# Maximum over the last axis of a 64 MB array: another division into loads, and another share for GpSimd

## The chip, the core and the metric

One core of a Trainium2 chip runs the kernel. The metric is the device time in microseconds (us) of one execution, as the median of several runs; lower is better. A profile of one execution, with a trace of every instruction and of every transfer, stands beside it.

## The reference

```python
# x: (32, 512, 1024) float32
def reference(x):
    return np.max(x, axis=-1).astype(np.float32)     # out: (32, 512)
```

The 32 x 512 vectors make 16384 rows of 1024 numbers, 67.1 MB in all; each gives one maximum. There is nearly nothing to compute per byte.

## The kernel before, in words

**Blocks and loads.** The 16384 vectors are cut into 128 blocks: a block puts one vector on each of the 128 partitions, 1024 numbers wide (512 KB). In this text a "row" of a load is one such block. `BLOCKS` (L13) divides the 128 rows into loads: a first list that sums to 112 rows, and a second whose sum is 14; the last two rows are loaded as four pieces (`PIECES`, L26, two column ranges for each of two rows). SyncE issues all of them in order on one queue (L238 and L243), into a ring of 47 rows in SBUF (`RING`, L17). A load is issued once everything that reads the rows it overwrites stands in the program ahead of it, and on the chip it waits until these reads are done. Loads are numbered from 0; load 10, for instance, is the one of 7 rows.

**VectorE** does most of the work: `maximum` (L78) is one reduce along the columns. Step `dK` reduces the rows of load K that VectorE keeps for itself, straight into the result columns.

**GpSimd's share.** For a few rows near the end the columns are turned, so that GpSimd can take the maximum over the partitions. `SHARED` (L20) says for a load K: (m, parts), so of its last m rows the first `parts` column-blocks of 128 go this other way. A chunk holds as many rows as fit eight column-blocks. Step `tN` handles chunk N: TensorE transposes each 128x128 block into PSUM (L160), ScalarE copies the result to SBUF (L166), GpSimd takes the maximum over the partitions (L168). Step `bN` turns the first partition's row back into columns with TensorE (L178). Where `parts` is below 8, step `pK` lets VectorE reduce the remaining columns of those rows beside it, in PSUM, and step `mK` takes the maximum of both. The loads named in `RANK` (L22) share one PSUM tile, `joint`, with one merge at the end (`m99`): so that each row of `joint` has as many columns, `partial` (L194) splits the remaining columns of a row into `s` segments and leaves one maximum for each. `joint` is as wide as its widest load needs: `parts`, plus one where `parts` is below 8.

**The end.** Steps `f0` to `f3` reduce the four pieces; the second piece of a row takes the result of the first in with it. Then `m99`. Results of the first 112 rows are stored once `f0` is done, the last 16 after `m99`.

**Order.** `PLAN` (L31) is the order of all steps, written out by hand. `in_turn` (L71) makes each engine keep it. Pools hold two buffers each for the transposes in PSUM, for their copies and for GpSimd's results, so chunk N waits for buffers of chunk N-2; the tile `joint` also makes TensorE and VectorE wait for one another where both write it.

Of the kernel before, what the change touches and what calls it, by code (L numbers as in the profile page):

```python
# [8 lines left out]
F32 = mybir.dt.float32  # L9

BLOCKS = [  # L13
    [2, 15, 16, 14, 11, 11, 10, 10, 8, 8, 7],
    [3, 3, 3, 2, 1, 1, 1],
]
RING = 47  # L17


SHARED = {10: (3, 8), 13: (2, 3), 14: (2, 3), 17: (1, 2)}  # L20

RANK = {13: 1, 14: 2, 17: 2}  # L22

PIECES = [(532, 492), (592, 432)]  # L26

PLAN = """  # L31
    d0 d1 d2 d3 d4 d5 d6 d7 d8 d9 t0 d10 t1 t2 d11 b0 d12 b1 d13 t3 p13 b2 p14 t4 m10 d15 b3
    d16 p17 t5 f0 b4 f1 f2 b5 f3 m99
""".split()

NOSYNC = mybir.DependencyInfo(mybir.DependencyClass.NoSync, mybir.DependencyReason.DATA)
# [4 lines left out]
def kernel(  # L41
# [35 lines left out]
    def maximum(out, in_):  # L77
        return in_turn("DVE", nc.vector.reduce_max(out=out, in_=in_, axis=X))  # L78
# [20 lines left out]
    for sizes in BLOCKS:  # L99
# [7 lines left out]
        b, place = 0, {}  # L107
        for i in sorted(range(len(sizes)), key=lambda i: RANK.get(base + i, 0)):
            place[i] = b
# [8 lines left out]
    assert first == I  # L118
    shared = [SHARED.get(j, (0, C)) for j in range(len(loads))]

    lead = [0 if RANK.get(j) == 3 else n - m for j, ((_, n, _, _), (m, _)) in enumerate(zip(loads, shared))]
    final = [j for j in range(len(loads)) if j in RANK]
    final.sort(key=lambda j: loads[j][3])
# [11 lines left out]
    def rows(j):  # L135
        start, n, _, _ = loads[j]
        return ring[:, I + start * D:I + (start + n) * D].rearrange("p (i d) -> p i d", d=D)
# [4 lines left out]
    def share(j):  # L142
        m, parts = shared[j]
        if j in RANK:
            r = loads[j][3] + lead[j] - col0
            return joint[:, r:r + m, :]
        if j not in fetched:
            got = psmall.tile([P, m, parts + (parts < C)], F32)
            fetched[j] = got
        return fetched[j]  # L150
# [39 lines left out]
    def partial(j):  # L190
        m, parts = shared[j]

        s = width - parts if j in RANK else 1
        maximum(share(j)[:, :, parts:], rows(j)[:, lead[j]:lead[j] + m, parts * P:].rearrange(  # L194
# [102 lines left out]
```

## Time and profile before

| what | value |
| --- | --- |
| median of 3 runs | 163.71 us (163.69 to 163.97) |
| span of the profiled execution, first to last instruction | 162.1 us |
| VectorE busy | 135.3 us (83%), 33 instructions |
| GpSimd busy | 15.9 us (10%), 10 instructions, of them 6 reductions over partitions |
| TensorE matmul busy | 13.6 us (8%), 76 instructions |
| ScalarE busy | 6.3 us (4%) |
| loads and stores | 67.18 MB, 414 GB/s over the span |
| mean granted TensorE clock | 0.955 |

The page gives no time of its own for the profiled execution beside the span; the 1.6 us between span and median lie outside the span.

How to read it: a row of a group names the line, the engine, the operation, output and input with their shapes, and after the bar the busy time in us, the mean of one instruction in ns, and the idle time of the engine just before, with what ended it. The chain of waits follows the work that ended last back in time: each piece has its start, its length and its place. A stretch view gives the busy time of each engine between two moments.

### The profile page before, as it was taken

To read this page: it belongs to the slowest core of one execution; us is meant where nothing else is said; L and a number is where in the kernel's file an instruction comes from. 1 tells how busy PE (TensorE), PEld (TensorE's weight loads), DVE (VectorE), ACT (ScalarE), POOL (GpSimd) and SP (SyncE) were. 2 spreads that over 40 slices of the span, in tenths; PEclk is the share of its full clock that TensorE was granted. 3 is DMA by queue.
4 is the path that set the end of the run, shared out by engine and by line. 5 is a ranking of instruction groups with operands and counts; after the bars stand their busy time and mean duration, and the time that the engine had idled before them with its cause. 6 is when DMAs were issued, how large, how long until landed. Compare 5 with 4: busy or idle time off the path is not lost.

```text
span 162.1 us, 295 instructions
## 1 busy us (share of the span) xinstructions
PE 13.6 (8%) x76; PEld 11.7 (7%) x76; DVE 135.3 (83%) x33; ACT 6.3 (4%) x7; POOL 15.9 (10%) x10
## 2 busy tenths in 40 slices
PE   0000000000000000000000000000000000772942
PEld 0000000000000000000000000000000000762731
DVE  3500019998399999999999999996999999999994
ACT  3000000000000000000000000000000000241120
POOL 0000000000000000000000000000000000099791
PEclk9999999999999999999999999999999999996555
DMA  5995999599879999898999799799999989999991
GB/s 178 566 485 258 470 501 517 259 517 517 354 340 439 453 404 534 356 523 367 478 411 475 334 485 475 334 485 388 477 429 388 466 382 446 415 421 416 411 388 34
DMA packets 3456, 67.18 MB, mean 414 GB/s; under 512 B 640, under 2 KB 896, under 8 KB 1536
## 3 DMA queue, kind: packets, MB, share of 16 engines
q1 hardware_dynamic: 3168, 67.11, 96.8%
q10 hardware_dynamic: 288, 0.07, 0.2%
HBM read 67.11 MB, written 0.07 MB: 414 GB/s over the span
## 4 chain that ended last, share of the span: by engine, by line
DMA 50%; DVE 47%; SPq 1%; issue 0%; DVEq 0%
DMA ring<-in_x_dram 50%; DVE ring L78 45%; DVE joint L78 2%; SPq L238 1%; DVEq L292 0%
## 5 line engine op out<-in xcount | busy, mean ns | idle before, releaser
L78 DVE TENSOR_REDUCE ring<-ring 128x1 f32<-128x1024 f32 (+13 forms) x20 | 129.9, 6547 | 23.5 <-DMA ring<-in_x_dram 23.5
L168 POOL PARTITION_ALL_REDUCE top<-sb x6 | 15.7, 2658 | 142.6 <-ACT sb L166 142.5
L160 PE MATMUL ps<-ident,ring 128*128 128x128 f32 x38 | 9.0, 423 | 140.0 <-DMA ring<-in_x_dram 140.0
L160 PEld LDWEIGHTS ps<-ident,ring 128*128 128x128 f32 x38 | 7.6, 225 | 140.1 <-issue 140.1
L166 ACT COPY sb<-ps 128x1024 f32<-128x1024 f32 (+2 forms) x6 | 5.0, 834 | 150.5 <-PE ps L160 143.5
L78 DVE TENSOR_REDUCE joint<-ring 128x2 f32<-128x1280 f32 (+1 forms) x3 | 3.9, 1314 | 0.0
L178 PE MATMUL got<-ident,top 1*128 1x1 f32 x24 | 2.7, 228 | 3.8 <-POOL top L168 3.6
L178 PEld LDWEIGHTS got<-ident,top 1*128 1x128 f32 x24 | 2.4, 188 | 4.6 <-POOL top L168 4.6
L178 PE MATMUL joint<-ident,top 1*128 1x1 f32 x14 | 2.0, 244 | 1.9 <-POOL top L168 1.9
L178 PEld LDWEIGHTS joint<-ident,top 1*128 1x128 f32 x14 | 1.7, 210 | 2.7 <-POOL top L168 2.7
L166 ACT ACT_TABLE_LOAD x1 | 1.3, 1283 | 0.7 <-PEq L281 0.7
L83 DVE MEMSET ident<- 128x128 f32 x1 | 0.2, 165 | 0.8 <-PEq L281 0.8
L90 DVE TENSOR_SCALAR rowno<-rowno 32x1 f32<-32x1 f32 x3 | 0.4, 146 | 0.1
L85 DVE TENSOR_TENSOR_SCAN colno<-ident 128x128 f32<-128x128 f32 x1 | 0.4, 425 | 0.0
L92 DVE TENSOR_SCALAR ident<-colno,rowno 128x128 f32<-128x128 f32 x1 | 0.3, 288 | 0.0
L87 DVE STREAM_TRANSPOSE rowno<-colno 128x32 f32<-128x32 f32 x1 | 0.2, 211 | 0.0
L78 DVE TENSOR_REDUCE ring<-got 128x3 f32<-128x24 f32 x1 | 0.2, 172 | 0.0
L78 DVE TENSOR_REDUCE ring<-joint 128x5 f32<-128x20 f32 x1 | 0.2, 170 | 0.0
L281 POOL MEMSET const-float32-0.0<- 128x1 f32 x1 | 0.1, 98 | 0.2 <-issue 0.2
L281 POOL MEMSET const-bfloat16-1.0<- 128x1 bf16 x1 | 0.1, 102 | 0.0
L281 POOL MEMSET const-uint8-127<- 128x1 uint8 x1 | 0.1, 101 | 0.0
L281 POOL MEMSET const-float32-1.0<- 128x1 f32 x1 | 0.1, 98 | 0.0
(1 smaller groups left out, 0.1 us busy)
## 6 DMA issues: line engine op xcount, KB each, us to landing
ring<-in_x_dram SPq DMA_DIRECT2D x2, 5632.0 KB, 29.9
ring<-in_x_dram SPq DMA_DIRECT2D x2, 5120.0 KB, 36.8
ring<-in_x_dram SPq DMA_DIRECT2D x2, 4096.0 KB, 32.5
ring<-in_x_dram SPq DMA_DIRECT2D x1, 7680.0 KB, 22.6
ring<-in_x_dram SPq DMA_DIRECT2D x1, 7168.0 KB, 58.0
ring<-in_x_dram SPq DMA_DIRECT2D x3, 1536.0 KB, 35.7
ring<-in_x_dram SPq DMA_DIRECT2D x1, 3584.0 KB, 29.2
ring<-in_x_dram SPq DMA_DIRECT2D x2, 1024.0 KB, 17.8
```

The lines of the kernel that those rows point to most:

```text
L78: return in_turn("DVE", nc.vector.reduce_max(out=out, in_=in_, axis=X))
L83: in_turn("DVE", nc.vector.memset(ident, 1.0))
L85: in_turn("DVE", nc.vector.tensor_tensor_scan(out=colno, data0=ident, data1=ident, initial=-1.0, op0=ALU.add, op1=ALU.mult))
L87: in_turn("DVE", nc.vector.transpose(out=rowno, in_=colno[:, :32]))
L90: in_turn("DVE", nc.vector.tensor_scalar(out=part, in0=part, scalar1=float(q * 32), scalar2=None, op0=ALU.add))
L92: identity = in_turn("DVE", nc.vector.tensor_scalar(out=ident, in0=colno, scalar1=rowno[:, 0:1], scalar2=None, op0=ALU.is_equal))
L160: in_turn("PE", nc.tensor.transpose(out=ps[:, w:w + P], in_=rows(j)[:, lead[j] + r + i, c * P:(c + 1) * P], identity=ident,))
L166: in_turn("ACT", nc.scalar.copy(out=sb[:, :W], in_=ps[:, :W]))
L168: in_turn("POOL", nc.gpsimd.partition_all_reduce(top[:, :W], sb[:, :W], P, bass_isa.ReduceOp.max))
L178: in_turn("PE", nc.tensor.transpose(out=share(j)[:, r + i, c:c + 1], in_=tops[k][0:1, w:w + P], identity=ident[0:1, 0:1],))
L238: load = nc.sync.dma_start(out=rows(issued), in_=src)
L281: nc = _bacc.Bacc("TRN2", target_bir_lowering=False, num_devices=1)
```

## The change

The first list has 10 loads for 11: it starts with 16 rows where there were 2, and ends with 2. The second has 7 loads as before, in other sizes. With the four pieces, 21 transfers stand for 22. GpSimd's share goes from four loads (3x8, 2x3, 2x3 and 1x2 column-blocks, 38 in all) to five (5x3, 4x3, 1x8, 2x3 and 1x2, 43 in all), in eight chunks for six. Load 8, with 8 rows, keeps 3 rows for VectorE alone and has a merge of its own; loads 10, 11, 13 and 16 go to `joint`, which becomes 8 rows of 8 (it was 5 rows of 4), since load 11 shares all eight column-blocks of one row. The segments per row in `partial` become 5, 5 and 6 (they were 1, 1 and 2). The functions stay as they are; ring, pieces and pools too.

In the built program TensorE has 86 transposes (it had 76) and SyncE 21 loads and pieces (22); VectorE has 32 instructions that compute (33).

```diff
 BLOCKS = [
-    [2, 15, 16, 14, 11, 11, 10, 10, 8, 8, 7],
-    [3, 3, 3, 2, 1, 1, 1],
+    [16, 14, 16, 14, 12, 11, 10, 9, 8, 2],
+    [4, 3, 2, 2, 1, 1, 1],
 ]
 RING = 47
-SHARED = {10: (3, 8), 13: (2, 3), 14: (2, 3), 17: (1, 2)}
-RANK = {13: 1, 14: 2, 17: 2}
+SHARED = {8: (5, 3), 10: (4, 3), 11: (1, 8), 13: (2, 3), 16: (1, 2)}
+RANK = {10: 2, 11: 1, 13: 2, 16: 2}
 PIECES = [(532, 492), (592, 432)]
 PLAN = """
-    d0 d1 d2 d3 d4 d5 d6 d7 d8 d9 t0 d10 t1 t2 d11 b0 d12 b1 d13 t3 p13 b2 p14 t4 m10 d15 b3
-    d16 p17 t5 f0 b4 f1 f2 b5 f3 m99
+    d0 d1 d2 d3 d4 d5 d6 d7 d8 t0 t1 t2 p8 b0 d9 t3 b1 p10 b2 t4 t5 m8 d11 b3 d12 b4 p13 t6 d14
+    b5 d15 p16 t7 f0 b6 f1 f2 b7 f3 m99
 """.split()
```

## The prediction, made before the changed kernel ran

> **What bounds the kernel now.** I read the slices of the page first: how busy are the transfers?
>
> ```profile
> span 162.1 us, 295 instructions
> ...
> DMA  5995999599879999898999799799999989999991
> ...
> q1 hardware_dynamic: 3168, 67.11, 96.8%
> q10 hardware_dynamic: 288, 0.07, 0.2%
> ```
>
> The transfers look full with dips. The slices can't say whether a dip is real, so I asked for stretches cut at landings (columns: stretch, its length, busy time and count of PE, PEld, DVE, ACT, POOL, then clock, DMA share, GB/s):
>
> ```profile
> 5.60:23.80 18.20, 0.00 (x0) 0.00 (x0) 2.30 (x2) 0.00 (x0) 0.00 (x0) 1.00 1.01 436
> 23.80:43.10 19.30, 0.00 (x0) 0.00 (x0) 16.14 (x1) 0.00 (x0) 0.00 (x0) 1.00 0.99 428
> 43.10:111.00 67.90, 0.00 (x0) 0.00 (x0) 66.57 (x6) 0.00 (x0) 0.00 (x0) 1.00 0.99 427
> 111.00:139.00 28.00, 0.03 (x1) 0.06 (x1) 27.98 (x3) 0.00 (x0) 0.00 (x0) 1.00 1.00 429
> 139.00:150.00 11.00, 6.93 (x40) 6.42 (x40) 10.96 (x5) 3.04 (x3) 7.95 (x3) 0.89 1.00 422
> ```
>
> The DMA share is 0.99 to 1.01 everywhere: the dips come from packets that straddle slices. **The stream of loads is one unbroken line from the first load to the last piece.** VectorE is nearly as full from 43 us on. The chain of waits shows both:
>
> ```profile
> 1.62 41.49 DMA ring<-in_x_dram
> ...
> 43.13 66.55 DVE ring L78 x5
> ...
> 111.01 38.94 DMA ring<-in_x_dram
> 149.95 0.02 issue
> 149.97 1.22 DVE ring L78
> ...
> 158.57 0.49 DVE ring L78
> 159.05 0.09 issue
> 159.14 0.59 DVE ring L78
> ```
>
> The chain hops between two lines that are both late. After 149.97 it is all VectorE, but the last two piece reduces (158.57, 159.14) follow a landing by about 0.1 us as well.
>
> **The price of a load.** Landings: load 2 (16 rows) at 1.62 + 41.49 = 43.11, load 13 at 111.01 + 38.94 = 149.95; load 1 at 23.76 (VectorE, which waits for it, starts at 23.78, as it starts at 43.13 on load 2). Load 2 takes 19.35 us for 16 rows and one load. From there to load 13 it is 106.84 us for 88 rows and 11 loads. With a per row and b per load, 16a + b = 19.35 and 88a + 11b = 106.84, so a = 1.2047 and **b = 0.075 us**. Load 0 (2 rows) lands at 5.62, so the stream starts, as it were, at 5.62 - 2.48 = 3.14. Before's total, 3.14 + 128 x 1.2047 + 22 x 0.075 = 158.99, meets the last landing (150.0 + 9.0, the last issue's time to landing).
>
> A rule to weigh: the Trainium skill, "DMA: Bandwidth & Descriptors", section "Anatomy of one DMA", gives each DMA a fixed cost of some 2.0 us. By that rule one load fewer would save 2 us. The rows above show it overlapped when loads queue up, so the measured 0.075 is used.
>
> **The stream after the change.** 21 transfers for 22, the bytes unchanged: the last landing moves **by -0.075 us** if the stream stays unbroken. With the same start the 16 rows of the first load land at 22.5, loads 1 to 8 at 39.4, 58.8, 75.7, 90.2, 103.6, 115.7, 126.6 and 136.3, the rest at 138.8, 143.7, 147.4, 149.9, 152.3, 153.6, 154.9, 156.2, the pieces at about 156.9, 157.7, 158.4 and 158.9.
>
> Does a refill come too late? Each load waits for VectorE to leave its rows of the ring. Load 3 waits for reduce 0 (39.7), behind it lies load 2 until 58.8; load 4 for reduce 1 (54.7), behind load 3 until 75.7; loads 5 and 6 for reduce 2 (76.0), with load 4 until 90.2; load 7 for reduce 3 (91.0), with loads 5 and 6 until 115.7; loads 8 to 11 for reduce 4 (103.9); 12 and 13 for reduce 5 (115.7). The least cover is 14 us. The last three loads and the pieces wait for older loads to land; the tightest, the fourth piece, for load 12 at 149.9, with 8 us queued. So the stream holds.
>
> **VectorE.** Its rows:
>
> ```profile
> L78 DVE TENSOR_REDUCE ring<-ring 128x10 f32<-128x10240 f32 x2 | 21.6, 10821 | 1.3 <-DMA ring<-in_x_dram 1.3
> L78 DVE TENSOR_REDUCE ring<-ring 128x1 f32<-128x1024 f32 x3 | 3.6, 1213 | 0.0
> L78 DVE TENSOR_REDUCE joint<-ring 128x2 f32<-128x1280 f32 x2 | 3.0, 1490 | 0.0
> L78 DVE TENSOR_REDUCE joint<-ring 128x2 f32<-128x768 f32 x1 | 1.0, 961 | 0.0
> L78 DVE TENSOR_REDUCE ring<-got 128x3 f32<-128x24 f32 x1 | 0.2, 172 | 0.0
> ```
>
> 1024 more elements cost (10821 - 1213)/9 = 1067.6 ns, 0.96 elements a nanosecond, plus 0.15 us; a queued instruction starts some 0.085 us before the one ahead ends (five of 17.22 + 15.08 + 23.75 + 10.82 = 66.87 fill 66.53). The change removes 5 of 128 column-blocks of 1/8 row, 0.67 us, and starts VectorE's large work at 22.5 for 23.8, but takes away the 2.3 us done at 5.65. In sequence: reduces 0 to 5 end at 39.7, 54.7, 76.0, 91.0, 103.9, 115.7; 6 and 7 wait 0.1 to 0.2 us for landings and end at 126.5 and 136.4. Then load 8: 3 rows 3.35, the share of 5 x 640 columns 3.49; 2 rows 2.28 (145.3); 4 x 640 2.83 (148.0); the merge 0.17; 2 rows twice (152.5). The share of load 13 can start at 152.46, as its load lands (152.3 plus the semaphore); 1.5, 1.21, 1.21, then load 16's share at 156.3, bound by its landing, 0.96; the pieces' two reduces at 157.2 and 157.8; the last two at 158.5 and 159.07, bound by landings. So VectorE catches up with the stream at 115.7, 126.6, 152.4, 156.2 and the end: **the stream sets the end, with VectorE 0.0 to 0.2 us behind cover.** The last merge reads 8 x 8 for 5 x 4 values: 44 more, +0.046 us at the very end.
>
> Shares now leave segments of 128 columns apart: outputs of 4 x 5, 2 x 5 and 6 for 2, 2 and 2, 30 more. No row shows five segments per row. Bounds: the 128x768 row has two segments in one row and takes 0.80 + 0.161, the 128x1280 row two rows and 1.333 + 0.157, so nothing (0.00); at most the whole residue of the 128x24 row per output, (172 - 25)/3 = 49 ns, that is 1.5 us. I take 0, the row nearest in form.
>
> A rule against the change: the Trainium skill, "VectorE: DVE Perf Modes", section "The TRN2 errata", lets one large tile pay the exposed memory latency once and many small tiles each, and advises tiles of 512 elements or more. Were a segment such a tile, at the page's 58 cycles (60 ns) 30 of them would add an estimated 1.8 us; the 128x768 row, with its two segments at no more than the fixed cost of one instruction, speaks against that reading, and no run here shows five.
>
> **TensorE, ScalarE, GpSimd.** Eight chunks for six. GpSimd rows: 1024 columns 3.2 to 3.3 us, 768 columns 2.50, 256 columns 1.12; 384 lies between, about 1.47. Copies: 1.01, 0.80, 0.37; transposes 0.21 apart, from landing to copy 1.6 for six. GpSimd starts at 138.8 (load 8 at 136.3 + 1.6 + 0.8) and ends its two first chunks at 143.7. The third waits for the first columns to be turned back, and these for the share of load 8 (143.1): it runs 144.0 to 145.5. Then load 10's chunks 146.4 to 151.5, load 11's 1024 columns to 154.7, load 13's to 157.4, load 16's to 158.5. Turned back: by 158.9, and the last merge starts at 159.6. Two waits reach VectorE: load 13's share waits for load 10's columns (done 152.33, needed 152.4), load 16's for load 11's (155.7, needed 156.2). So this line is hidden, by 0.1 us in one place; a delay there is soaked up by the landing waits at 156.2 and 158.4, so the first 0.2 us cost nothing.
>
> **Sum:** -0.075 + 0.046 = -0.03 us on a span of 162.07, 162.04. The median of the runs is 163.71, 1.64 above the span, which I hold fixed: **163.68 us**. What a measurement of this kernel can tell from no change is about 0.2%, 0.33 us.
>
> **Rivals.**
> A, *the stream starts earlier.* The first transfer is now eight times larger. Before loses time at the start (363 GB/s in the first 5.6 us, 436 after); whether larger packets start closer together, no row shows. At 436 GB/s from the issue at 0.72, 2 rows (1.05 MB) would land at 3.1 for 5.62: a limit of -2.5 that nothing reaches; the other way, an issue of 0.61 (the longest row) for 0.37 makes +0.24. I take 0, the row of before; if a sixth of the limit is won, -0.4: 163.3.
>
> B, *slower by code loading.* TensorE gets ten more transposes (86 for 76, each two instructions) and three more waits, though its program is said to keep its length. The queue list of before shows data queues alone: no code arrives in the span. If the longer program needs one more fetch, its packets share 16 full engines, and each microsecond that one engine loses delays every later landing. Bounds: nothing, where it comes before the span, and the smallest whole load, 1 row in 1.28 us; I price it between a quarter and a half of that: +0.3 to +0.6, 164.0 to 164.3. It decides once a fetch falls between 2 and 158 us.
>
> C, *slower by segments.* At 10 ns each VectorE's last slack goes (+0.2), at 20 ns +0.6: 164.3; at the bound about 165.1.
>
> D, *GpSimd's line late.* Pulled 0.3 us longer per reduction, load 13's share waits and the end moves +0.25; at 0.5, +1.5: 165.2. All its widths but 384 have rows, so this is unlikely.
>
> That a load less isn't saved, because VectorE governs, is inside the forecast: then +0.05.
>
> **Chances.** Forecast (163.5 to 164.0) 0.75, A 0.09, B 0.06, C 0.06, D 0.04. Range 163.4 to 164.2: it holds the forecast, the near ends of A and C, and most of B; what is left out is under 0.2. Faster by over 0.2% is A, 0.09; slower B, C and D, 0.16; same 0.75.
>
> **What would show it.** In the profile after: DMA share 1.0 in every stretch; the first 16 rows at 22.5; the chain ending with piece reduces that follow landings near 158.4 and 158.9; a last landing 0.07 earlier; 4 x 5 x 128 at 2.8 us; no third queue in the list. A VectorE wait for PE before load 13's share speaks for D; a first landing before 22.3 for A.

## The result, and the profile after

The changed kernel takes 164.09 us (median of 21 runs, 163.93 to 164.23) where the kernel before, run beside it, takes 163.75 us (21 runs, 163.56 to 164.13). The ratio is 1.0019, with a 95% interval of 1.0013 to 1.0025: **0.31 us slower, 0.21 to 0.41**. The forecast was 163.68, a gain of 0.03.

The page of the changed kernel, its slices and its list of queues:

```profile
span 162.3 us, 324 instructions
...
DMA  7979999799996999999988989799899999999990
...
q1 hardware_dynamic: 3024, 67.11, 96.7%
q10 hardware_dynamic: 288, 0.07, 0.2%
```

The packets fell from 3168 to 3024: the change did what it says. No third queue appeared. The chain of waits (start, length, what) says where the time lies:

```profile
0.72 21.98 DMA ring<-in_x_dram
22.71 0.02 issue
22.73 32.21 DVE ring L74 x2
...
152.69 1.49 DVE joint L74
154.18 2.26 DVE ring L74 x2
...
156.53 0.96 DVE joint L74
157.50 1.14 DVE ring L74 x2
158.63 0.06 issue
158.69 0.47 DVE ring L74
159.17 0.10 issue
159.27 0.60 DVE ring L74
```

The first load lands at 0.72 + 21.98 = 22.70, where 22.49 was forecast (22.5 in its text). VectorE is already 0.2 us late there, with nothing done that it could have done wrong. The last piece reduce starts at 159.27 for 159.07 forecast: the same 0.2. **What was lost was lost in the first 22 us, and was neither won back nor added to in the 137 us after.** The waits of VectorE agree (waited for: us in total, times, longest):

```profile
DVE ring L74 <- DMA ring<-in_x_dram: 24.3, 2, 20.2
DVE ident L79 <- PEq L277: 0.8, 1, 0.8
```

The second line is the start of the program, 0.8 us in all; there is no wait for a result of TensorE or GpSimd. Two rows of the new forms, with busy time and mean:

```profile
L74 DVE TENSOR_REDUCE joint<-ring 128x20 f32<-128x2560 f32 x1 | 2.8, 2817 | 0.0
L74 DVE TENSOR_REDUCE joint<-ring 128x10 f32<-128x1280 f32 x1 | 1.5, 1494 | 0.0
...
L74 DVE TENSOR_REDUCE ring<-joint 128x8 f32<-128x64 f32 x1 | 0.2, 214 | 0.0
```

2817 ns is 2560/0.96 + 150: twenty segments of 128 cost nothing over the length. The last merge takes 214 ns for 170, +0.044, as computed.

In what follows the *start of the stream* is a worked-out number: the landing of the first load less 1.2047 us per row and 0.075 for the load. Before: 5.62 - 2.48 = 3.14. After: 22.71 - 19.35 = 3.36.

### The profile page after: what moved, and what is told of

Read it like the earlier page. It is cut to its first block, busy times and chain, and to the rows that moved or that the text cites. A ratio compares the mean times of both kernels' runs of the same rounds, so it can differ in the third digit from the quotient of the medians.

```text
span 162.3 us, 324 instructions
## 1 busy us (share of the span) xinstructions
PE 15.8 (10%) x86; PEld 13.6 (8%) x86; DVE 134.5 (83%) x32; ACT 7.1 (4%) x9; POOL 18.4 (11%) x12
## 3 DMA queue, kind: packets, MB, share of 16 engines
q1 hardware_dynamic: 3024, 67.11, 96.7%
## 4 chain that ended last, share of the span: by engine, by line
DVE 59%; DMA 35%; another core or an unknown queue 2%; issue 1%; DVEq 0%
DVE ring L74 54%; DMA ring<-in_x_dram 35%; DVE joint L74 3%; DVE got L74 2%; DVEq L288 0%; DVEq L74 0%
## 5 line engine op out<-in xcount | busy, mean ns | idle before, releaser
L74 DVE TENSOR_REDUCE ring<-ring 128x2 f32<-128x2048 f32 (+12 forms) x18 | 124.5, 6960 | 24.4 <-DMA ring<-in_x_dram 24.3
L164 POOL PARTITION_ALL_REDUCE top<-sb x8 | 18.2, 2298 | 140.2 <-ACT sb L162 139.8
L156 PE MATMUL ps<-ident,ring 128*128 128x128 f32 x43 | 10.4, 425 | 137.3 <-DMA ring<-in_x_dram 137.3
L156 PEld LDWEIGHTS ps<-ident,ring 128*128 128x128 f32 x43 | 8.5, 223 | 137.5 <-issue 137.4
L162 ACT COPY sb<-ps 128x768 f32<-128x768 f32 (+3 forms) x8 | 5.9, 733 | 149.8 <-PE ps L156 148.5
L74 DVE TENSOR_REDUCE joint<-ring 128x20 f32<-128x2560 f32 (+2 forms) x3 | 5.3, 1757 | 0.1
L174 PE MATMUL joint<-ident,top 1*128 1x1 f32 x28 | 3.8, 244 | 2.7 <-POOL top L164 2.7
L174 PEld LDWEIGHTS joint<-ident,top 1*128 1x128 f32 x28 | 3.3, 211 | 4.0 <-POOL top L164 3.7
L74 DVE TENSOR_REDUCE got<-ring 128x5 f32<-128x3200 f32 x1 | 3.5, 3484 | 0.0
L174 PE MATMUL got<-ident,top 1*128 1x1 f32 x15 | 1.9, 241 | 3.4 <-DVE got L74 3.4
```

The source lines that it names most:

```text
L156: in_turn("PE", nc.tensor.transpose(out=ps[:, w:w + P], in_=rows(j)[:, lead[j] + r + i, c * P:(c + 1) * P], identity=ident,))
L162: in_turn("ACT", nc.scalar.copy(out=sb[:, :W], in_=ps[:, :W]))
L164: in_turn("POOL", nc.gpsimd.partition_all_reduce(top[:, :W], sb[:, :W], P, bass_isa.ReduceOp.max))
L174: in_turn("PE", nc.tensor.transpose(out=share(j)[:, r + i, c:c + 1], in_=tops[k][0:1, w:w + P], identity=ident[0:1, 0:1],))
```

## The experiments

Two theories went in. **S**: the stream starts later when its first load has large packets. (One packet carries what one partition gets: 8 KB in a load of 2 rows, 64 KB in one of 16.) **T**, the rival: the cost sits in the changed tail. Each timing below stands beside runs of the kernel before in the same session; their medians were 163.68, 163.72 and 163.73 us.

| kernel | first load, rows | transfers | median us | ratio to before (95%) | start of the stream |
| --- | --- | --- | --- | --- | --- |
| before | 2 | 22 | 163.75 | | 3.14 |
| before, again | 2 | 22 | 163.70 | 1.0004 (0.9995 to 1.0013) | 2.91 |
| before, 1 and 16 | 1 | 22 | 163.71 | 1.0008 (0.9998 to 1.0017) | 3.23 |
| before, 8 and 9 | 8 | 22 | 163.85 | 1.0012 (1.0003 to 1.0021) | 3.01 |
| before, 16 and 1 | 16 | 22 | 163.96 | 1.0013 (1.0005 to 1.0022) | 3.20 |
| changed | 16 | 21 | 164.09 | 1.0019 (1.0013 to 1.0025) | 3.36 |
| changed, again | 16 | 21 | 164.02 | 1.0020 (1.0011 to 1.0028) | 3.36 |
| changed, 8 and 8 | 8 | 22 | 163.84 | 1.0004 (0.9995 to 1.0013) | 3.09 |
| changed, 2 and 14 | 2 | 22 | 163.73 | 1.0005 (0.9996 to 1.0013) | 2.82 |
| changed, 1 and 15 | 1 | 22 | 163.81 | 1.0011 (1.0002 to 1.0021) | 2.95 |
| changed, other source | 16 | 21 | 164.05 | 1.0016 (1.0007 to 1.0025) | 3.46 |
| changed, small transfer ahead | 16 | 22 | 164.68 | 1.0055 (1.0042 to 1.0067) | 3.90 |
| changed, the same from ScalarE | 16 | 22 | 164.03 | 1.0017 (1.0008 to 1.0026) | 3.42 |

The start in the last column is that of one profiled execution, and moves by 0.2 us between two of the same kernel; the time is that of five to twenty-one. The rerun of the kernel before shows what a ratio can say here: about 0.1% up or down.

**1. Only the first load's size, in the kernel before.** Loads 0 and 1, 17 rows together, are cut in another place; count, tail and GpSimd's share stay.

```diff
-    [2, 15, 16, 14, 11, 11, 10, 10, 8, 8, 7],
+    [16, 1, 16, 14, 11, 11, 10, 10, 8, 8, 7],
```

> The kernel before with its first two loads of 2 and 15 rows cut as 16 and 1: as many transfers, the same tail. Theory S (the stream starts later when the first load has packets of 64 KB): the seventeenth row lands 0.1 to 0.3 us later than the 23.76 of before, every landing after it too, and the time is 0.15 to 0.35 us above before. Theory T (the cost sits in the tail of the changed kernel: wider joint, segments, longer GpSimd line): no change, within 0.08 us of before.

Measured 163.96, +0.28 us by the medians, 0.08 to 0.36 by the ratio. The profiled execution has its seventeenth row at 23.81 for 23.76, less than expected, but the 2 rows of that first profile had come late (3.14); the second profile of before has it at 23.51. T is out as the main cause: the tail is the old one.

Another rival is VectorE: with 16 rows first it has nothing to do for 22 us, and loses the reduce of 2 rows that before had done by 7.9. But it has caught up at 43.19, for there it waits 2.27 us for a landing again:

```profile
43.19 17.22 DVE L78 TENSOR_REDUCE ring<-ring 128x16 f32<-128x16384 f32 x1 [2.27 <-DMA ring<-in_x_dram]
```

**2. The sizes between.** The same line, with 8 and 9 rows, and with 1 and 16:

```diff
+    [8, 9, 16, 14, 11, 11, 10, 10, 8, 8, 7],
...
+    [1, 16, 16, 14, 11, 11, 10, 10, 8, 8, 7],
```

> The kernel before with first loads of 8 and 9 rows (packets of 32 KB). Theory S: between before and the 16-and-1 kernel, +0.05 to +0.2 us; if the delay came from any first load over 2 rows alike, as much as with 16. Theory T: within 0.08 us of before.

> The kernel before with first loads of 1 and 16 rows (packets of 4 KB). Theory S: as before or slightly faster, 0 to -0.1 us, the seventeenth row landing at 23.65 to 23.76. Theory T: within 0.08 us of before.

8 rows: +0.17 us by medians, between the two, as S has it. 1 row: +0.03, no gain over 2 rows that can be measured. Its profiled execution took 164.27, near the longest of its set: the first landing came late (start 3.23; the seventeenth row landed at 23.82, where 23.65 to 23.76 was expected), and about 0.3 us more were lost in the last part of the stream.

**3. The changed kernel with a small first load.** Here everything of the change stays except its first load, and the 22nd transfer returns.

```diff
-    [16, 14, 16, 14, 12, 11, 10, 9, 8, 2],
+    [2, 14, 14, 16, 14, 12, 11, 10, 9, 8, 2],
```

(Numbers of loads in `SHARED`, `RANK` and `PLAN` move by one, and `PLAN` gets a `d0` ahead.)

> The changed kernel with its first load of 16 rows cut into 2 and 14; everything behind is the same, one more transfer. Theory S: the start of before is back, minus its delay of about 0.25 us, plus 0.075 for the transfer, plus 0.05 for the wider last merge: 0 to 0.1 us above before, and 0.15 to 0.3 below the changed kernel. Theory T: the tail's cost stays and the transfer is added: 0.35 to 0.45 us above before.

Measured 163.73 us beside 163.68: +0.05 by the medians, where the changed kernel stands 0.30 and 0.34 above before in its two sets of runs. **One transfer more makes the changed kernel faster by about 0.3 us, and takes the slowdown away**, as far as the interval can tell (0.9996 to 1.0013). T had 164.03 to 164.13.

> The changed kernel with its first load cut into 1 and 15 rows (packets of 4 KB first), one more transfer. Theory S: as the cut into 2 and 14, -0.1 to +0.1 us against before. Theory T: +0.35 to +0.45 us.

1 and 15 rows: 163.81, at the upper end of what S expected. With 1 and with 2 rows first the times can't be told apart.

> The changed kernel with its first load cut into 8 and 8 rows (packets of 32 KB), one more transfer. By the size of the first packets: the start lies between those of 2 and 16 rows, as with 8 and 9 rows in the kernel before: +0.1 to +0.25 us against before. If only 64 KB packets cost: 0.0 to +0.1 us.

8 and 8 rows: 163.84, +0.11 by the medians; the interval of the ratio holds no change as well. So 64 KB is clear, and 32 KB lies between without being settled alone; the two 8-row kernels together lean to a small cost.

**4. Both kernels once more, for second profiles.**

> The kernel before once more, for a second profile of it: how far single executions differ. Theory S (delay at the start of the stream, by the size of the first packets): time within 0.1 us of before; the first 2 rows land between 5.2 and 5.7, and the end follows that landing. Theory T (cost in the tail): the same time, and the start no later or earlier than in the changed kernel once the rows are allowed for.

> The changed kernel once more, for a second profile. Theory S: +0.25 to +0.4 us, the first 16 rows landing at 22.55 to 22.75 again (a stream that starts at 3.2 to 3.4 after 19.35 us for the load are taken off), the tail as computed. Theory T: +0.25 to +0.4 us with a VectorE wait for TensorE or GpSimd in the last 20 us.

Both times came as S had them: 163.70, and 164.02 beside 163.72, with the 2 rows landing at 5.39 and the 16 rows at 22.71. T's sign, a wait of VectorE for TensorE or GpSimd in the last 20 us, isn't there.

The stretch from 1.7 to 2.7 us holds the start of each engine's first packet. A packet is counted in the stretch where it starts, with its whole length, so the DMA share can exceed 1. The changed kernel, first profile:

```profile
1.70:2.70 1.00, 0.00 (x0) 0.00 (x0) 0.72 (x4) 0.30 (x1) 0.00 (x0) 1.00 3.07 1049
```

The kernel before with 16 and 1 rows, the same stretch:

```profile
1.70:2.70 1.00, 0.00 (x0) 0.00 (x0) 0.72 (x4) 0.30 (x1) 0.00 (x0) 1.00 3.06 1049
```

1049 GB/s for 1 us are sixteen packets of 65536 bytes, one for each engine, and a share of 3.07 means that they took 3.07 us on average. Later packets of 64 KB take 2.42 in the trace. **So a first packet of 64 KB overruns by 0.65 us on average**, from 0.0 to 0.95 us among the sixteen engines; in the second profile of the changed kernel it is 0.58. First packets of 8 KB overrun too: over the whole first load an engine lost 0.42 to 0.51 us with 8 KB packets and 0.57 to 0.66 with 64 KB. The large packets thus cost the average engine only some 0.2 us more, an estimate from these records. Much of the rest of the later landing lies in the slowest engine: it ends the first load 0.20 to 0.28 us behind the average one with 8 KB packets and 0.29 to 0.42 with 64 KB.

VectorE's first waits show what follows from it: the second profile of before, then that of the changed kernel:

```profile
5.41 2.29 DVE L78 TENSOR_REDUCE ring<-ring 128x2 f32<-128x2048 f32 x1 [2.90 <-DMA ring<-in_x_dram]
23.53 16.15 DVE L78 TENSOR_REDUCE ring<-ring 128x15 f32<-128x15360 f32 x1 [15.83 <-DMA ring<-in_x_dram]
```

```profile
22.73 32.22 DVE L74 TENSOR_REDUCE ring<-ring 128x16 f32<-128x16384 f32 x2 [20.22 <-DMA ring<-in_x_dram]
59.00 17.22 DVE L74 TENSOR_REDUCE ring<-ring 128x16 f32<-128x16384 f32 x1 [4.06 <-DMA ring<-in_x_dram]
```

Seventeen rows and two loads by 23.51 in the one; sixteen rows and one load by 22.71 in the other, that is 1.28 less work in only 0.80 us less. The end of the chain of both, before first:

```profile
158.35 0.48 DVE ring L78
158.84 0.10 issue
158.94 0.60 DVE ring L78
```

```profile
158.72 0.46 DVE ring L74
159.17 0.12 issue
159.29 0.59 DVE ring L74
```

0.35 us between the last reduces: 0.45 of the start (3.36 less 2.91), less 0.075 for the transfer, would be 0.375.

**5. Is it where the first packets read?** The 16 rows of the first load come from 2048 vectors that lie next to each other, and the 16 result columns are those of other vectors than the reference's.

```diff
+            if issued == 0:
+                src = xf[:n * P, :].rearrange("(p i) d -> p i d", p=P)
             load = nc.sync.dma_start(out=rows(issued), in_=src)
```

> The changed kernel, but the first load reads 2048 vectors that lie next to each other in memory (64 KB from one partition's data to the next, for 448 KB); its 16 rows of results are those of other vectors. If the late start comes from the size of the packets: as the changed kernel, +0.25 to +0.4 us, first landing at 22.55 to 22.75. If it comes from where the first packets read (all engines 448 KB apart): the start of before is back, +0.0 to +0.1 us, first landing near 22.4.

Measured 164.05, start 3.46, first landing 22.82: the delay stays. It isn't the distance of 448 KB between the partitions' data.

**6. Is it a waking up that any first packet would pay?** A transfer of 256 bytes per partition goes ahead.

```diff
+    primer = once.tile([P, 64], F32)
+    nc.sync.dma_start(out=primer, in_=xf[0:P, 0:64])
```

> The changed kernel with a small transfer ahead of the 16-row load on the same queue: 64 columns of 128 vectors (256 B per partition) into a place that nobody reads. If the late start is paid once per engine by whatever packet comes first (an engine that has to wake up): the start of before is back, about 0.3 us won, less 0.1 to 0.2 us for the transfer and for the issue of the big load that comes 0.42 us later: -0.2 to 0.0 us against the changed kernel. If it comes with the size of the first large packets, however they are preceded: the delay stays and the transfer is added, +0.1 to +0.4 us against the changed kernel, +0.4 to +0.7 against before.

Measured 164.68, 0.95 above before and beyond even the dear end of the expectation. In the trace the small packets start from 1.73 us on, on all engines, and take their 0.02 us without any overrun; the 64 KB packets behind them start from 2.20 us, since their load is issued 0.42 us later, and still overrun, by 0.60 us on average (0.08 to 1.11). Of the 0.95 us, 0.31 are the changed kernel's, and 0.54 are seen in the trace as a later first landing (VectorE starts at 23.27 for 22.73), of which some 0.45 is the later start of the large packets (2.46 on average for 2.00); the last 0.1 isn't explained. So engines that have just moved a packet lose as much, if the stream has run dry in between, as it had here.

Large packets that follow without a break lose next to nothing. In the changed kernel with 2 and 14 rows first, the stretch from 4.6 us on holds the first packets of the second load, 56 KB each, and the last two of 8 KB:

```profile
4.60:5.60 1.00, 0.00 (x0) 0.00 (x0) 0.28 (x1) 0.00 (x0) 0.00 (x0) 1.00 2.18 934
```

The sixteen of 56 KB took 2.13 us on average, and 2.12 is what such packets take later.

The same transfer from ScalarE's queue, so that the big load needn't be issued later:

```diff
+    nc.scalar.dma_start(out=primer, in_=xf[0:P, 0:64])
```

> The changed kernel with the same small transfer, but issued on ScalarE's queue, so that the 16-row load is issued as early as in the changed kernel. Woken engines: -0.2 to -0.05 us against the changed kernel. Size of the packets: 0.0 to +0.1 us against the changed kernel, +0.3 to +0.4 against before.

164.03, start 3.42, which reads like a delay by the size of the packets, but the trace takes its worth away: the small packets moved at 4.8 us and later, behind the first large ones. It primed nothing, and tells only that such a transfer costs little.

## Why the prediction was wrong, point by point

**The bound was right.** One stream of transfers sets the end: the lateness of the first landing (0.22 against the forecast) stands unchanged at the last reduce (0.20).

**The price of a load was right.** Landings of the changed kernel lie at the forecast ones plus 0.17 to 0.26 us all the way (39.62 for 39.4, 75.91 for 75.7, 138.99 for 138.8, 156.41 for 156.2), so 0.075 per load and 1.2047 per row hold, and no refill came late. (The 2.0 us that the prediction weighs against it stand in a section on transfers that GpSimd issues; here SyncE issues the loads.)

**VectorE was right**, lateness apart: the share of load 8 took 3.48 (3.49), that of load 10 2.82 (2.83), and load 13's share could start at 152.68, 0.12 us after its landing at 152.56. The segments (C) cost nothing; the rule on small tiles, read as one per segment, doesn't hold here: the row of twenty segments has no time over its length and the fixed 150 ns.

**GpSimd's line was right**, nearest at load 13's share as said: the last of load 10's columns was turned back at 152.54, 0.14 us ahead of the share's start. Rival D didn't occur. Code loading (B) didn't either: no third queue in the list.

**The step that failed** is "with the same start the 16 rows of the first load land at 22.5", and with it rival A, "I take 0, the row of before". A looked for a stream that starts earlier. It starts later. The bound on that side, +0.24, was taken from the length of an issue instruction, which was in fact 0.36 us for 0.37 and had nothing to do with it. Measured between profiles of the two kernels it is +0.22 to +0.45. The sum mended: the start 3.36 less 3.03 (mean of the two profiles of before) is +0.33, the transfer -0.075, the merge +0.044: +0.30, where 0.31 was measured. That it comes so near is partly luck, since the two profiles of before differ by 0.23 themselves. The first transfer meets an empty stream, as no other does. The row of before for it has 8 KB packets and was no row for 64 KB packets: the cost was not shown by the trace, and should have been bounded as such, on the slower side too.

**A second term was mis-sized.** The sum adds 1.64 us to a span of 162.07, as the time outside the span, and holds that fixed. No view shows 162.07: the page has 162.1, the trace 162.10. And in all twelve runs whose profiled execution has its own time on record, that time is 1.77 to 1.78 above its span (163.67 and 161.89 for before, 164.10 and 162.33 for the changed kernel). So the profiled execution of before took an estimated 163.88 us, 0.17 above the median, and the start of 3.14 in it was a late one. Of the 0.41 us between the forecast and the measured 164.09, this term makes 0.13. The other 0.29 is the span, 162.33 for 162.04: 0.2 of that is the start, 0.03 the wrong reading, and the rest stands behind the last reduce.

That 164.09 lies in the stated range, 163.4 to 164.2, is luck: its upper part was there for B and C, and neither occurred.

**What stays open.** Why a larger packet loses more when it starts on an idle stream. The overrun was read off the records and moved with the size; the source's layout, and a waking up that any packet would pay, were excluded as causes, no mechanism was shown. In all these kernels a load of more rows has larger packets, 128 of them each time, so whether the packet's size or the load's counts was not separated. A small transfer that keeps the stream busy right up to the large packets, without a cost of its own, wasn't tried. No kernel here beats the one before: the changed kernel with a small first load has as many transfers again, and equals it.

## What to carry to other kernels

A kernel that is one unbroken stream of transfers pays whatever happens to the first packets in full, because nothing later can win it back (here 0.22 us at the first landing and 0.20 at the last reduce). Its first load should be small (1 or 2 rows here, for 16), for the stream's sake and not only for the engine that waits for it; count what a saved transfer is worth from the spacing of landings in the queue (here 0.075 us), and compare it with what the transfer did at the start. And where a step is said to stay as it was, look whether the instruction that carries it still has the same shape.

## What the runs showed of the hardware that was not expected

The first packet of each of the sixteen DMA engines takes longer than the same packet later: 0.65 us at 64 KB (3.07 for 2.42) in the first profile of the changed kernel. Counted over all packets of the first load, an engine lost 0.35 us at 4 KB (two profiles), 0.42, 0.46 and 0.51 at 8 KB, 0.56 and 0.67 at 32 KB, and 0.57 to 0.66 at 64 KB (0.79 with the other source), each from one profiled execution. So most of the loss is paid whatever the size, and the size adds to it.

The engines also end apart, and stay so. Each engine closes a load with a packet of 4 bytes. In the first load these sixteen lie 0.3 to 0.5 us apart with 8 KB packets and 0.6 to 0.9 with 64 KB (but 0.55 and 0.96 with 4 KB, so size isn't all of it). In the changed kernel the spread of 0.62 is still 0.58 at the last piece, and its first load lands at 22.71, 0.35 after the last of the sixteen (22.36), so the slowest engine sets the landing.

A stream that has started well can still lose time on the way. The profiled execution of the changed kernel with 2 and 14 rows started at 2.82, the earliest of all, and ran as late as the changed kernel at the end. VectorE's waits in it show where (idle before in brackets):

```profile
115.64 10.82 DVE L74 TENSOR_REDUCE ring<-ring 128x10 f32<-128x10240 f32 x1 [0.22 <-DMA ring<-in_x_dram]
126.85 13.06 DVE L74 TENSOR_REDUCE ring<-ring 128x9 f32<-128x9216 f32 x2 [0.39 <-DMA ring<-in_x_dram]
```

Load 8 (9 rows) came 11.21 us after the one ahead, for 10.92 by the price above. That execution took 164.08 us, where the median of the kernel is 163.73: one profile isn't the kernel's usual time, and the medians decided here.
